# Shared keys and values of a hybrid decoder trunk: seven products of quarters (Strassen's scheme) in place of eight

## The chip, the cores and the metric

The kernel runs on 1 core of one Trainium2 chip. The metric is the device time of one launch in microseconds, median of several runs. A core has TensorE (PE, matrix products into PSUM banks), VectorE (DVE), ScalarE (ACT) and GpSimd (POOL) for elementwise work, and SyncE (SP), whose queue issues the DMA transfers here.

## The reference, cut to what matters

One HGRN2 layer updates the residual stream x; then the keys and values, shared by the FoX attention layer, are computed from it. The change lies in `h @ kv_w` (1024 x 1024 times 1024 x 4112; WIDTH is 2048, 16 heads of 128).

```python
def _shared_kv(x, c, kv_mod_w, kv_mod_b, kv_norm_g, kv_w, kv_fb, k_norm_g):
    ...
    h = _rms(x, kv_norm_g) * (1.0 + scale[:, None]) + shift[:, None]
    proj = h @ kv_w
    k = proj[..., :WIDTH].reshape(bsz, s, B_HEADS, HEAD_DIM)
    v = proj[..., WIDTH:2 * WIDTH].reshape(bsz, s, B_HEADS, HEAD_DIM)
    fl = proj[..., 2 * WIDTH:] + kv_fb
    k = _rms(k, k_norm_g).transpose(0, 2, 1, 3)
    ...
    F = jnp.cumsum(jax.nn.log_sigmoid(fl.astype(jnp.float32)), axis=1).transpose(0, 2, 1)
    return k, v, F
```

## The kernel before, in words

Every large float32 product is made of float32r halves: an operand is split into hi (ScalarE copies it with rounding, L224) and lo (VectorE or GpSimd subtracts hi from it, L225), and hi.hi + hi.lo + lo.hi are three matmuls into one bank. `halves` does both. On chip there are 25 blocks of 128 x 2048 floats, each of two halves of 1024; `renew` gives a block a new life, `ar(b, off, n)` names a piece.

The order of TensorE's work is written out by hand in a class `Weave`: matmuls are chained in the order in which the program issues them, `tick` counts a made-up time, and `spawn` lays side jobs (transposes and what follows) in when that time has come; `need(mark)` runs a side job at once. The other engines take their instructions in the order of a scheduler, SP's DMA queue too.

The stages: norm and HGRN2 with its input products; `out_proj`, which gives row tile t of the new residual stream in `a_done`; the shared keys and values; FoX attention with its own input products; a second `out_proj`. `a_done(t)` (L785) adds the residual row, stores it to x1d, squares it (L798), takes the root with a dozen small VectorE operations (`rsqrt_mean`, L213 to L219) and scales it on GpSimd (L800). `x_turn(t)` (L766), laid in 12 us of made-up time later, transposes the row tile in eight matmuls, stores it to xnd (L775), modulates it on VectorE (L776, L777) and splits it into halves in `hT`.

The stage in question is the loop over p (L873): for each of eight pairs of heads the products of k (four tiles of two row blocks, `gemm_N`, 24 matmuls of 128 x 256 per row block) and of v. k is read from its bank twice (L886, L888), squared sums are reduced (L887), the root taken, k scaled (L891), and `k_turn` transposes it and stores it to kd. v is copied (L902) and stored to vd. Weights are split one product set ahead by `split_w`, on GpSimd. For p = 0 the forget gate's 32 matmuls and its side job `forget_sums` follow. For the last p, `b_h` (L863) loads the transposed rows again from xnd, scales them on GpSimd (L868) and splits them anew as the operands of the FoX layer's products; those begin with L952, whose first tile is squared (L957), reduced (L959) and scaled (L961) before its transposes (`q_turn`). Names in the trace: blk is a block, mm, oa and sm are the three kinds of PSUM banks.

## Time and profile before

| what | value |
|---|---|
| median of 3 runs | 2383.89 us (2381.35 to 2388.03) |
| the profiled execution, its own time | 2386.32 us |
| its span | 2384.6 us |
| mean granted TensorE clock | 0.988 |
| TensorE busy | 96% of the span |
| VectorE, ScalarE, GpSimd busy | 58%, 42%, 25% |
| stage of shared keys and values | from about 1142.8 to 1548 us of the span |

The span is from the first to the last instruction of the execution; its own time holds 1.7 us more around it. In a timeline a row gives start, length, engine, line and operation; in brackets how long the engine stood idle before and what released it. A matmul's own length is longer than its pace, since matmuls overlap.

### The profile page before, as it was taken

To read this page: it belongs to the slowest core of one execution; us is meant where nothing else is said; L and a number is where in the kernel's file an instruction comes from. 1 tells how busy PE (TensorE), PEld (TensorE's weight loads), DVE (VectorE), ACT (ScalarE), POOL (GpSimd) and SP (SyncE) were. 2 spreads that over 40 slices of the span, in tenths; PEclk is the share of its full clock that TensorE was granted. 3 is DMA by queue.
4 is the path that set the end of the run, shared out by engine and by line. 5 is a ranking of instruction groups with operands and counts; after the bars stand their busy time and mean duration, and the time that the engine had idled before them with its cause. 6 is when DMAs were issued, how large, how long until landed. Compare 5 with 4: busy or idle time off the path is not lost.

```text
span 2384.6 us, 38476 instructions
## 1 busy us (share of the span) xinstructions
PE 2300.3 (96%) x14760; PEld 2063.2 (87%) x14760; DVE 1373.1 (58%) x3587; ACT 1004.1 (42%) x1646; POOL 587.4 (25%) x511
## 2 busy tenths in 40 slices
PE   4999999999999999999999999999999999999999
PEld 3888888888878798788999999989999999998887
DVE  7565555665656566647661131367767766777533
ACT  5453444434353526334422222344544545446321
POOL 3222222222222221101322121333333334333000
PEclk9999999999999999999999999999999999999999
DMA  8313131313222233666423232422222322235443
GB/s 270 102 40 103 45 97 45 97 53 98 63 80 75 77 94 98 200 198 190 147 82 94 71 95 84 141 67 74 81 80 67 94 70 91 66 95 173 155 142 117
DMA packets 219964, 244.95 MB, mean 103 GB/s; under 512 B 14546, under 2 KB 182644, under 8 KB 219780
## 3 DMA queue, kind: packets, MB, share of 16 engines
q1 hardware_dynamic: 219780, 242.49, 32.6%
q8 instruction: 116, 1.90, 0.3%
q14 instruction: 68, 0.56, 0.1%
HBM read 196.22 MB, written 46.21 MB: 102 GB/s over the span
## 4 chain that ended last, share of the span: by engine, by line
PE 82%; DVE 9%; ACT 4%; DMA 2%; issue 2%; POOL 1%; SPq 0%; DVEq 0%; ACTq 0%; POOLq 0%
PE mm L48 65%; PE oa L48 6%; PE sm L48 6%; PE sm L51 5%; DVE dl L471 1%; DVE blk L225 1%; DMA blk<-in_b_w_out_dram 1%; ACT L464 1%; DVE blk L465 1%; DVE rs_t L214 1%; ACT blk L224 1%; DVE blk L263 1%; ACT blk L464 0%; DVE blk L853 0%; POOL blk L225 0%
## 5 line engine op out<-in xcount | busy, mean ns | idle before, releaser
L48 PE MATMUL mm<-blk,blk 128*128 128x256 f32 (+1 forms) x10688 | 1916.0, 334 | 8.4 <-ACT blk L224 4.3
L48 PEld LDWEIGHTS mm<-blk,blk 128*128 128x128 f32 x10688 | 1604.0, 191 | 182.0 <-ACT blk L224 6.7
L224 ACT ACTIVATE blk<-blk 128x1024 fp32r<-128x1024 f32 (+3 forms) x352 | 304.8, 881 | 391.2 <-PE mm L48 251.3
L225 POOL TENSOR_TENSOR blk<-blk,blk 128x1024 fp32r<-128x1024 f32 (+1 forms) x134 | 312.6, 2343 | 569.5 <-ACT blk L224 567.0
L225 DVE TENSOR_TENSOR blk<-blk,blk 128x1024 fp32r<-128x1024 f32 (+3 forms) x218 | 204.2, 944 | 191.6 <-ACT blk L224 180.0
L48 PE MATMUL oa<-blk,blk 128*128 128x256 f32 (+1 forms) x1248 | 186.6, 286 | 25.2 <-DVE blk L515 14.7
L51 PE MATMUL sm<-ident,blk 128*128 128x128 f32 x1201 | 185.9, 275 | 23.7 <-DMA blk<-in_x_dram 9.8
L48 PE MATMUL sm<-blk,blk 128*128 128x128 f32 (+5 forms) x1408 | 207.5, 304 | 0.0
L48 PEld LDWEIGHTS oa<-blk,blk 128*128 128x128 f32 x1248 | 170.5, 194 | 36.7 <-DVE blk L515 16.0
L51 PEld LDWEIGHTS sm<-ident,blk 128*128 128x128 f32 x1201 | 142.6, 140 | 51.0 <-issue 20.2
L48 PEld LDWEIGHTS sm<-blk,blk 128*128 128x128 f32 (+1 forms) x1408 | 164.6, 171 | 19.6 <-issue 3.4
L1042 ACT ACTIVATE blk<-blk,m 128x128 f32<-128x128 f32 (+7 forms) x128 | 99.0, 773 | 128.2 <-DVE m L1040 115.8
L887 DVE TENSOR_REDUCE sst<-blk 128x4 f32<-128x512 f32 x32 | 21.8, 682 | 215.4 <-ACT blk L886 215.4
L1044 POOL TENSOR_SCALAR blk<-blk,smx 128x128 f32<-128x128 f32 (+7 forms) x128 | 97.6, 763 | 136.4 <-DVE smx L1043 117.3
L225 DVE TENSOR_TENSOR blk<-sm,blk 128x512 fp32r<-128x512 f32 (+1 forms) x160 | 93.0, 581 | 62.2 <-ACT blk L224 61.6
L263 DVE SCALAR_TENSOR_TENSOR blk<-blk,cc,blk 128x256 f32<-128x256 f32 x196 | 111.9, 573 | 20.2 <-DMA blk<-in_mod_w_dram 13.2
L1014 POOL TENSOR_TENSOR blk<-rows4k,keep 128x128 f32<-128x128 f32 x128 | 61.4, 479 | 238.2 <-DVE mx L1021 208.9
L545 POOL TENSOR_TENSOR blk<-blk,blk 128x512 f32<-128x512 f32 x32 | 43.0, 1344 | 237.8 <-ACT blk L544 210.4
L224 ACT ACTIVATE blk<-sm 128x512 fp32r<-128x512 f32 (+1 forms) x160 | 81.1, 507 | 46.9 <-PE sm L51 46.1
L1021 DVE CUSTOM_DVE_ANT_0 blk<-sm,rows4k 128x128 f32<-128x128 f32 (+3 forms) x176 | 84.7, 495 | 22.8 <-PE sm L48 21.4
L466 POOL TENSOR_SCALAR blk<-blk,cc 128x512 f32<-128x512 f32 x32 | 22.8, 712 | 260.0 <-ACT blk L463 253.4
L479 ACT ACT_TABLE_LOAD x31 | 39.8, 1283 | 102.4 <-DVE blk L474 102.4
(156 smaller groups left out, 1662.0 us busy)
## 6 DMA issues: line engine op xcount, KB each, us to landing
...
ogd<-blk SPq DMA_DIRECT2D x128, 64.0 KB, 1.8
...
```

The lines of the kernel that those rows point to most:

```text
L48: self._chain(self.PE.matmul(*a, **k))
L51: self._chain(self.PE.transpose(*a, **k))
L214: V.tensor_scalar(t.bitcast(I32), m.bitcast(I32), 1, None, ALU.logical_shift_right)
L224: S.activation(hi, src, AF.Copy)
L225: eng.tensor_tensor(lo, src, hi.bitcast(F32), ALU.subtract)
L263: V.scalar_tensor_tensor(acc, rawk(rb, k), csil[:, k:k + 1], acc, ALU.mult, ALU.add)
L479: S.activation(lf[:, :, 1, :], lf[:, :, 1, :], AF.Exp)
L545: G.tensor_tensor(u["ogT"], u["ogT"], sg(j, th), ALU.mult)
L1014: G.tensor_tensor(nfm, nF[:, i * P:n], negm, ALU.add)
L1021: V.tensor_tensor_reduce(dst, src, add, 1.0, -3e38, ALU.add, ALU.max, mx[:, nm:nm + 1])
L1042: S.activation(l[:, 0:n], l[:, 0:n], AF.Exp, bias=m, accum_out=sm)
L1044: G.tensor_scalar(l[:, 0:n], l[:, 0:n], sm, 0.0, ALU.mult, ALU.add)
```

## The change

The eight pairs become eight groups of 512 columns, four of v and four of k (`GROUPS`). Rows, contraction and columns are halved, so a group is a 2 x 2 by 2 x 2 product of quarters, and each quarter product is 4 row tiles x 4 steps of contraction x 3 matmuls = 48 matmuls of the shape used before. Seven products with sums (m = 1 to 7) take the place of eight: on the left A11, A12, S2 = A21 + A22 - A11, S3 = A11 - A21, S1 = A21 + A22, A22, S4 = A12 - S2; on the right B11, B21, T2 = B22 - T1, T3 = B22 - B12, T1 = B12 - B11, B21 - T2, B22. Left operands are made once: A11 and A12 in `x_turn` as before, the others from the modulated rows (blocks 4 to 7) on VectorE and, for S3, on GpSimd, while the first group's products run. Right operands are made per group: the four subtractions on GpSimd, the split on ScalarE and VectorE, for step i + 1 at the head of step i, into one of two slots (three from step 21). Sums of products are made in the bank where they can be, and else while the bank is read (`st_read`): ScalarE copies product 1 to SBUF, VectorE adds it, or an earlier sum, to the bank that it reads.

Step 0 needs x_turn of tiles 3 and 6; x_turn 7 is laid in after 8 instead of 12 us of made-up time. The forget gate's matmuls follow the first group and use A11, A12, S1 and A22 with weights changed to match; its arithmetic runs on 128 partitions. `b_h` comes in four parts at steps 1 to 4 of the last group, and `place` renames the blocks for the FoX stage, so that its operands lie where the group's operands have been used up.

```diff
+    GROUPS = [(kind, g) for kind, g in zip("vkkvvkkv", (0, 0, 1, 1, 2, 2, 3, 3))]
+    ORDER = [[1, 2, 6, 7, 5, 4, 3]] + [[1, 6, 2, 7, 5, 4, 3]] * 7
+    STEPS = [(n, m) for n in range(8) for m in ORDER[n]]
+    AOPS = {1: (0, 1), 2: (2, 3), 6: (14, 15), 7: (16, 17), 5: (18, 19), 4: (21, 22), 3: (4, 6)}
+    RAWQ = [(13, 0), (9, 0), (9, 1), (13, 1), (12, 0), (12, 1)]
...
+    def st_raw(n, q):
+        b, h = RAWQ[(4 * n + q) % 6]
+        return pr(b, 1024 * h, 1024)
...
+    def st_slot(i):
+        b = (8, 10)[i % 2] if i < 21 else (10, 7, 8)[i % 3]
+        return pr(b, 0, 1024, F32R), pr(b, 1024, 1024, F32R)
...
+    def st_prep(i):
+        n, m = STEPS[i]
+        b11, b12, b22, b21 = [st_raw(n, q) for q in range(4)]
+        t1, t2 = pr(23, 0, 1024), pr(23, 1024, 1024)
+        if m == 6:
+            G.tensor_tensor(t1, b12, b11, ALU.subtract)
+            G.tensor_tensor(t2, b22, t1, ALU.subtract)
+        if m == 7:
+            G.tensor_tensor(b12, b22, b12, ALU.subtract)
+        if m == 4:
+            G.tensor_tensor(t2, b21, t2, ALU.subtract)
+        halves(V, *st_slot(i), {1: b11, 2: b21, 3: b22, 4: t2, 5: t1, 6: t2, 7: b12}[m])
+    def st_products(i, banks, tiles):
+        m = STEPS[i][1]
+        wh, wl = [c256(w) for w in st_slot(i)]
+        first, last = m in (1, 6, 5), m in (2, 4, 3)
+        for j in tiles:
+            ps = c256(banks[j // 2])[:, j % 2, :]
+            for k in range(4):
+                ah, al = [a[:, k % 2, :] for a in st_A(AOPS[m][k // 2], j * P, P)]
+                for x, (lh, rh) in enumerate(((ah, wh), (ah, wl), (al, wh))):
+                    start = first and j % 2 == 0 and k == 0 and x == 0
+                    stop = last and j % 2 == 1 and k == 3 and x == 2
+                    PE.matmul(ps, lhsT=lh, rhs=rh[:, k, :], start=start, stop=stop, skip_group_check=True)
+                PE.tick(0.36)
...
-            raws["todo"] = [wcol(kv_w, o + p * 256) for p in range(NP) for o in (0, W)]
-            raws["slots"], raws["n"] = [13, 12], 0
-            raw_load()
+            for q in range(4):
+                st_load(0, q)
         if (ch, t) == (1, 4):
-            wnext.append(split_w(V, more=False))
+            st_prep(0)
...
             S.activation(xT, pt, AF.Copy)
             dma(xnd[th][:, q * 4:q * 4 + 4, o:o + P], c128(xT))
             V.tensor_tensor(c128(full), c128(xT), spread(g1[:, q * 4:q * 4 + 4], 4, P), ALU.mult)
-            V.tensor_tensor(c128(full), c128(full), spread(mcol[:, 48 + q * 4:52 + q * 4], 4, P), ALU.add)
             for k2 in range(2):
-                b = th * 4 + q * 2 + k2
-                halves(V, c512(ar(b, 0, 1024, F32R))[:, :, o:o + P], c512(ar(b, 1024, 1024, F32R))[:, :, o:o + P],
-                       c128(full)[:, 2 * k2:2 * k2 + 2, :])
+                hf = c512(pr(4 + 2 * th + q, 1024 * k2, 1024))[:, :, o:o + P]
+                c = 48 + q * 4 + k2 * 2
+                V.tensor_tensor(hf, c128(full)[:, 2 * k2:2 * k2 + 2, :], spread(mcol[:, c:c + 2], 2, P), ALU.add)
+                if th == 0:
+                    halves(V, *st_A(2 * q + k2, o, P), hf)
         PE.marks.add(("hkv", t))
         yield 0.0
@@ -798,127 +870,239 @@
         S.activation(xn, rows[t % 2], AF.Square, accum_out=ss)
         r = rsqrt_mean(ss, 1, 1.0 / D)
         G.tensor_scalar(xn, rows[t % 2], r, 0.0, ALU.mult, ALU.add)
-        PE.spawn(x_turn(t, xn), 12.0)
+        PE.spawn(x_turn(t, xn), 12.0 if t < NT - 1 else 8.0)
...
+    def st_sums(o, n):
+        for kk in range(2):
+            def hf(b):
+                return c512(pr(b, 1024 * kk, 1024))[:, :, o:o + n]
+            V.tensor_tensor(hf(22), hf(6), hf(7), ALU.add)
+            V.tensor_tensor(hf(12), hf(22), hf(4), ALU.subtract)
+    def st_split(src, dst, o=0, n=512):
+        for kk in range(2):
+            halves(V, *st_A(dst[kk], o, n), c512(pr(src, 1024 * kk, 1024))[:, :, o:o + n])
...
+    def st_done(n, c, tiles):
+        kind, g = GROUPS[n]
+        p, ts = 2 * g + c % 10 - 1, [4 * (c // 10 - 1), 4 * (c // 10 - 1) + 2]
+        if kind == "v":
+            for t, res in zip(ts, tiles):
+                dma(vd[p][:, t:t + 2, :], c256(res))
+            return
+        ss = sml.tile([P, 8], F32, name="ss8")
+        for b, res in enumerate(tiles):
+            sq = pr(5, 512 * b, 512)
+            S.activation(sq, res, AF.Square)
+            V.tensor_reduce(ss[:, 4 * b:4 * b + 4], c128(sq), AX.X, ALU.add)
+        r = rsqrt_mean(ss, 8, 1.0 / P)
+        for b, res in enumerate(tiles):
+            V.tensor_tensor(c128(res), c128(res), spread(r[:, 4 * b:4 * b + 4], 4, P), ALU.mult)
+        PE.spawn(k_turn(p, ts, tiles), 9.0)
+    def st_read(i, banks):
+        n, m = STEPS[i]
+        r1, u2, u3 = [[pr(blk, o + 512 * b, 512) for b in range(2)] for blk, o in ((11, 0), (11, 1024), (20, 0))]
+        if m == 1:
+            for b in range(2):
+                S.activation(r1[b], banks[b], AF.Copy)
+            return
+        if m in (6, 7):
+            for b in range(2):
+                V.tensor_tensor((u2 if m == 6 else u3)[b], banks[b], r1[b], ALU.add)
+            return
+        c = {2: 11, 5: 22, 4: 21, 3: 12}[m]
+        tiles = [st_res(c, b) for b in range(2)]
+        for b in range(2):
+            if m == 2:
+                S.activation(tiles[b], banks[b], AF.Copy)
+            else:
+                V.tensor_tensor(tiles[b], banks[b], {5: u3, 4: r1, 3: u2}[m][b], ALU.add)
+        if m == 3:
+            sq_n[0] += 2
+        st_done(n, c, tiles)
...
+    def b_h(th, k0):
+        for k in range(k0, k0 + 4):
+            xr = pr((9, 13)[k // 2 % 2], 1024 + 512 * (k % 2), 512)
             dma(xr, xnd[th][:, k, :])
             G.tensor_scalar(xr, xr, g1[:, 8 + k:9 + k], mcol[:, 24 + k:25 + k], ALU.mult, ALU.add)
             halves(V, hT(th, k, 0), hT(th, k, 1), xr)
...
-    raw_load()
-    wk = wnext[0]
-    for p in range(NP):
-        wv = split_w()
-        sst = sml.tile([P, 16], F32, name="sst")
-        for t in range(0, NT, 2):
-            if p == 0:
-                PE.need(("hkv", t + 1))
-            ps = mm_ps()
-            gemm_N(ps, wk, t)
-            sq = unit((t // 2) % 2)
-            S.activation(sq, ps, AF.Square)
-            V.tensor_reduce(sst[:, t * 2:t * 2 + 4], c128(sq), AX.X, ALU.add)
-            S.activation(kr(t), ps, AF.Copy)
-        r = rsqrt_mean(sst, 16, 1.0 / P)
-        for t in range(0, NT, 2):
-            V.tensor_tensor(c128(kr(t)), c128(kr(t)), spread(r[:, 2 * t:2 * t + 4], 4, P), ALU.mult)
-        PE.spawn(k_turn(p, kr), 11.0 if p == 1 else 6.0)
-        if p == NP - 1:
+    LAST = len(STEPS) - 7
+    for i, (n, m) in enumerate(STEPS):
+        if i == 0:
+            PE.need(("hkv", 3))
+            PE.need(("hkv", 6))
+            st_prep(1)
+        if i >= 1:
+            st_prep(i + 1)
+        if i == 1:
+            st_sums(0, 384)
+            st_split(12, AOPS[6], 0, 384)
+        if i == 2:
+            PE.need(("hkv", 7))
+            st_sums(384, 128)
+            st_split(12, AOPS[6], 384, 128)
+            for kk in range(2):
+                G.tensor_tensor(pr(6, 1024 * kk, 1024), pr(4, 1024 * kk, 1024), pr(6, 1024 * kk, 1024), ALU.subtract)
+            st_split(6, AOPS[7])
+        if i == 3:
+            st_split(22, AOPS[5])
+            renew(22)
+        if i == 4:
+            st_split(7, AOPS[4])
+            for kk in range(2):
+                V.tensor_tensor(pr(5, 1024 * kk, 1024), pr(5, 1024 * kk, 1024), pr(12, 1024 * kk, 1024), ALU.subtract)
+            renew(4, 6)
+            st_split(5, AOPS[3])
+            fls = forget_weights()
...
+        if i == LAST + 1:
+            place.update(zip(range(25), (0, 1, 14, 15, 2, 3, 16, 17, 18, 19, 8, 10, 12, 13, 21, 22, 4, 6, 5, 7, 9, 23, 20,
+                                         11, 24)))
+            b_h(0, 0)
+        if i == LAST + 2:
+            b_h(0, 4)
+        if i == LAST + 3:
+            b_h(1, 0)
+        if i == LAST + 4:
             raws["todo"] = [wcol(bw, o + q * 256) for q in range(NP) for o in (0, W)]
-            raws["slots"], raws["n"] = [12], 0
+            raws["slots"], raws["n"], wn[0] = [12], 0, 0
             raw_load()
-        wk = split_w()
-        for t in range(0, NT, 2):
-            ps = mm_ps()
-            gemm_N(ps, wv, t)
-            vt = unit(4 + (t // 2) % 2)
-            S.activation(vt, ps, AF.Copy)
-            dma(vd[p][:, t:t + 2, :], c256(vt))
-            if p == NP - 1 and t in (2, 6):
-                b_h(t // 4)
...
+            b_h(1, 4)
+        if i == LAST + 5:
+            wk = split_w()
+        banks = st_banks(m)
+        st_products(i, banks, range(4))
+        st_read(i, banks)
+        if i == 6:
+            PE.spawn(forget_sums(forget_logits(fls)), 2.0)
     PE.drain()
```

TensorE at the entry of the stage, before: the last matmuls of the projection, x_turn 5, and the first products; then, 99 matmuls on, x_turn 6.

```order
L48 MATMUL mm<-blk_0_7655,blk_1_7660 128x512
L51 MATMUL sm<-ident,blk_1_118 128x128 x8
L48 MATMUL mm<-blk_0_85,blk_0_69 128x256
L48 MATMUL mm<-blk_0_87,blk_0_69 128x256
...
L48 MATMUL mm<-blk_0_85,blk_1_78 128x256
L51 MATMUL sm<-ident,blk_0_117 128x128 x8
L48 MATMUL mm<-blk_0_85,blk_0_77 128x256
```

The same place in the change:

```order
L48 MATMUL mm<-blk_0_7657,blk_1_7662 128x512
L51 MATMUL sm<-ident,blk_1_118 128x128 x8
L51 MATMUL sm<-ident,blk_0_117 128x128 x8
L48 MATMUL oa<-blk_0_85,blk_0_69 128x256
L48 MATMUL oa<-blk_1_86,blk_0_69 128x256
```

x_turn 6 has moved from behind 99 matmuls to ahead of the first one, next to x_turn 5.

GpSimd during the first group of the change (L872 is the scaling in a_done, L786 to L791 the right-hand subtractions of `st_prep`, L1059 S3):

```order
L872 TENSOR_SCALAR blk24_0_117<-blk23_0_115,rs_y_9118 128x1024
L786 TENSOR_TENSOR blk23_0_115<-blk9_0_8366,blk13_0_95 128x1024
L872 TENSOR_SCALAR blk24_1_118<-blk23_1_116,rs_y_9168 128x1024
L789 TENSOR_TENSOR blk9_0_8366<-blk9_1_8367,blk9_0_8366 128x1024
L787 TENSOR_TENSOR blk23_1_116<-blk9_1_8367,blk23_0_115 128x1024
L791 TENSOR_TENSOR blk23_1_116<-blk13_1_96,blk23_1_116 128x1024
L1059 TENSOR_TENSOR blk6_0_8362<-blk4_0_8358,blk6_0_8362 128x1024
L1059 TENSOR_TENSOR blk6_1_8363<-blk4_1_8359,blk6_1_8363 128x1024
```

Before, the scalings of tiles 5, 6 and 7 (L800) had the weight splits of the first v products (L225) among them; now the subtractions of the first group stand there, two of S3 last.

GpSimd at the exit, before (L868 is the scaling in `b_h`, L225 the split of the FoX weights, L1014 the first work of attention):

```order
L868 TENSOR_SCALAR blk23_1_116<-blk23_1_116,cc_177 128x512 x2
L225 TENSOR_TENSOR blk11_0_91<-blk12_0_93,blk10_0_89 128x1024
L868 TENSOR_SCALAR blk23_0_115<-blk23_0_115,cc_177 128x512
L225 TENSOR_TENSOR blk11_1_92<-blk12_1_94,blk10_1_90 128x1024
L868 TENSOR_SCALAR blk23_0_115<-blk23_0_115,cc_177 128x512
L868 TENSOR_SCALAR blk23_1_116<-blk23_1_116,cc_177 128x512 x2
```

And in the change (L1036 is the scaling in `b_h`, L233 the split of the FoX weights):

```order
L1036 TENSOR_SCALAR blk13_1_96<-blk13_1_96,cc_179 128x512 x2
L786 TENSOR_TENSOR blk23_0_115<-blk12_1_94,blk12_0_93 128x1024
L789 TENSOR_TENSOR blk12_1_94<-blk13_0_95,blk12_1_94 128x1024
L787 TENSOR_TENSOR blk23_1_116<-blk13_0_95,blk23_0_115 128x1024
L1036 TENSOR_SCALAR blk9_1_8367<-blk9_1_8367,cc_179 128x512 x2
L791 TENSOR_TENSOR blk23_1_116<-blk9_0_8366,blk23_1_116 128x1024
```

The scalings now begin among the last group's own subtractions and are all ahead of the FoX weights' splits; before, the last of them came after those of the first gate weight.

## Rows read from the trace of the kernel before

**Rows 1.** The page's part 1: busy time, share, instructions.
```profile
PE 2300.3 (96%) x14760; PEld 2063.2 (87%) x14760; DVE 1373.1 (58%) x3587; ACT 1004.1 (42%) x1646; POOL 587.4 (25%) x511
```

**Rows 2.** Busy time by stretch: stretch, length, PE, PEld, DVE, ACT, POOL, clock, DMA, GB/s.
```profile
1300.00:1350.00 50.00, 49.31 (x414) 49.11 (x413) 10.15 (x20) 14.47 (x22) 10.79 (x5) 1.00 0.27 85
...
1550.00:1575.00 25.00, 20.03 (x150) 19.81 (x150) 16.83 (x51) 7.16 (x14) 7.47 (x7) 0.86 0.20 63
```

**Rows 3.** Timeline of ScalarE, middle of the stage: reads of successive banks.
```profile
1306.04 0.60 ACT L886 ACTIVATE blk<-mm 128x512 f32<-128x512 f32 x1 [4.17 <-PE mm L48]
1311.80 0.60 ACT L886 ACTIVATE blk<-mm 128x512 f32<-128x512 f32 x1 [4.67 <-PE mm L48]
...
1354.74 0.60 ACT L886 ACTIVATE blk<-mm 128x512 f32<-128x512 f32 x1 [4.17 <-PE mm L48]
```

**Rows 4.** Timeline of TensorE at the entry of the stage.
```profile
1142.02 1.03 PE L51 MATMUL sm<-ident,blk 128*128 128x128 f32 x8
1142.82 12.12 PE L48 MATMUL mm<-blk,blk 128*128 128x256 f32 x99
1154.77 1.04 PE L51 MATMUL sm<-ident,blk 128*128 128x128 f32 x8
```

**Rows 5.** Timelines of VectorE and GpSimd at the entry: the norms of tiles 5 to 7.
```profile
1145.74 0.69 DVE L790 TENSOR_TENSOR blk<-blk,rows4k 128x512 f32<-128x512 f32 x1 [2.77 <-DMA blk<-in_x_dram]
...
1149.02 2.39 DVE L219 SCALAR_TENSOR_TENSOR rs_y<-rs_t,rs_y 128x1 f32<-128x1 f32 x1
...
1135.93 2.40 POOL L225 TENSOR_TENSOR blk<-blk,blk 128x1024 fp32r<-128x1024 f32 x1 [9.39 <-ACT blk L224]
...
1148.65 2.73 POOL L225 TENSOR_TENSOR blk<-blk,blk 128x1024 fp32r<-128x1024 f32 x1 [7.10 <-ACT blk L224]
1153.51 1.12 POOL L800 TENSOR_SCALAR blk<-blk,rs_y 128x1024 f32<-128x1024 f32 x1 [2.12 <-DVE rs_y L215]
```

**Rows 6.** Timelines of GpSimd and VectorE where both work at once.
```profile
1139.19 1.48 POOL L800 TENSOR_SCALAR blk<-blk,rs_y 128x1024 f32<-128x1024 f32 x1 [0.85 <-DVE rs_y L219]
...
1168.93 4.82 POOL L225 TENSOR_TENSOR blk<-blk,blk 128x1024 fp32r<-128x1024 f32 x2 [5.36 <-ACT blk L224]
...
1139.82 0.69 DVE L789 TENSOR_TENSOR rows4k<-mm,rows4k 128x512 f32<-128x512 f32 x1
...
1169.86 0.69 DVE L887 TENSOR_REDUCE sst<-blk 128x4 f32<-128x512 f32 x1 [1.98 <-ACT blk L886]
...
1171.40 2.37 DVE L214 TENSOR_SCALAR rs_t<-rs_m 128x16 int32<-128x16 int32 x1
```

**Rows 7.** Groups by line and form from 1250 to 1500 us: count, busy us, mean ns, idle before.
```profile
L225 POOL TENSOR_TENSOR blk<-blk,blk 128x1024 fp32r<-128x1024 f32 x22 | 52.4, 2405 | 184.5 <-ACT blk L224 184.5
L224 ACT ACTIVATE blk<-blk 128x1024 fp32r<-128x1024 f32 x23 | 24.3, 1057 | 35.7 <-PE mm L48 22.6 <-issue 13.1
```

**Rows 8.** Timeline of VectorE: a split of 1024, of 256 columns, and two small operations.
```profile
1122.47 0.42 DVE L225 TENSOR_TENSOR blk<-blk,blk 128x256 fp32r<-128x256 f32 x1
...
1124.32 1.23 DVE L225 TENSOR_TENSOR blk<-blk,blk 128x1024 fp32r<-128x1024 f32 x1
...
1328.11 0.17 DVE L217 SCALAR_TENSOR_TENSOR rs_t<-rs_y 128x16 f32<-128x16 f32 x1
1328.32 0.17 DVE L218 TENSOR_TENSOR rs_t<-rs_t,rs_m 128x16 f32<-128x16 f32 x1
```

**Rows 9.** Waits from 1145 to 1560 us: total, times, longest.
```profile
PE sm L51 <- DVE blk L891: 6.1, 8, 1.4
```

**Rows 10.** Timelines of TensorE and VectorE at the exit of the stage.
```profile
1562.39 1.08 PE L51 MATMUL sm<-ident,blk 128*128 128x128 f32 x4 [4.97 <-DVE blk L961]
1563.13 7.66 PE L48 MATMUL mm<-blk,blk 128*128 128x256 f32 x48
...
1570.98 5.92 PE L48 MATMUL mm<-blk,blk 128*128 128x256 f32 x39
...
1557.78 0.69 DVE L225 TENSOR_TENSOR blk<-blk,blk 128x512 fp32r<-128x512 f32 x1 [0.16 <-ACT blk L224]
```

More of the change, by code (lines that the diff above doesn't have):

```diff
@@ L104, in renew, with pr @@
             i, js = i if isinstance(i, tuple) else (i, (0, 1))
+            i = place.get(i, i)
             for j in js:
                 blocks[i, j] = arena.tile([P, 1024], F32, tag=f"blk{i}_{j}", name=f"blk{i}_{j}")
-    renew(*range(25))
-    def ar(b, off, n, dt=F32):
+    place = {}
+    def pr(b, off, n, dt=F32):
         t = blocks[b, off // 1024]
@@ L116, in ar @@
         return t[:, off:off + n]
+    renew(*range(25))
+    def ar(b, off, n, dt=F32):
+        return pr(place.get(b, b), off, n, dt)
     def unit(u, n=512, dt=F32):
@@ L136, in hybrid_trunk_kernel @@
     Fd = drm.tile([H, T], F32, name="Fd")
+    zd = [drm.tile([P, P], F32, name=f"zd{i}") for i in range(2)]
     gd = [drm.tile([KT, P], F32, name=f"gd{l}") for l in range(2)]
@@ new lines, in forget_logits @@
+    def forget_logits(fls):
+        pf = [sm_ps(), sm_ps()]
+        for th, terms in enumerate(([(k, (0, 1, 2, 3)[k // 2], k) for k in range(8)],
+                                    [(k, (18, 19)[k // 2], k) for k in range(4)]
+                                    + [(8 + k, (21, 22)[k // 2], k) for k in range(4)])):
+            for x, (w, blk, k) in enumerate(terms):
+                for lo in range(2):
+                    PE.matmul(pf[th][0:48, :], lhsT=fls[:, w, :], rhs=st_A(blk, 0, 512)[lo][:, k % 2, :],
+                              start=(x + lo == 0), stop=(x + lo == 8))
+                PE.tick(0.46)
+        return pf
@@ L839, in forget_sums @@
+        dma(zd[0].rearrange("(h s) q -> h (s q)", h=H), z0)
+        z, e, a, s2, acc = [rows4k[:, i * P:(i + 1) * P] for i in range(5)]
+        dma(z, zd[0])
         yield 20.0
@@ L842, in forget_sums @@
         S.activation(e, e, AF.Exp)
[L843 removed]
+        V.tensor_scalar(a, e, 1.0, 2.0, ALU.mult, ALU.add)
+        V.reciprocal(a, a)
         yield 3.0
[L845 to L847 removed]
         V.tensor_tensor(a, a, e, ALU.mult)
         V.tensor_tensor(s2, a, a, ALU.mult)
[L850 removed]
         V.tensor_scalar(acc, s2, 1.0 / 17, None, ALU.mult)
@@ L853, in forget_sums @@
             V.scalar_tensor_tensor(acc, acc, 1.0 / n, s2, ALU.add, ALU.mult)
-            yield 3.0
+        yield 3.0
         V.scalar_tensor_tensor(acc, acc, 1.0, a, ALU.add, ALU.mult)
         V.tensor_scalar(z, z, -1.0, 0.0, ALU.mult, ALU.max)
-        yield 3.0
         V.scalar_tensor_tensor(z, acc, 2.0, z, ALU.mult, ALU.add)
+        dma(zd[1], z)
+        renew((7, (0,)))
+        one, out_f = pr(7, 0, 1024)[0:H, :], rows4k[0:H, :]
         G.memset(one, 1.0)
-        V.tensor_tensor_scan(e, one, z, 0.0, ALU.mult, ALU.add)
-        dma(Fd, e)
-    def b_h(th):
-        for k in range(KT):
-            xr = unit(20 + k % 4)
+        dma(z0, zd[1].rearrange("(h s) q -> h (s q)", h=H))
+        yield 10.0
+        V.tensor_tensor_scan(out_f, one, z0, 0.0, ALU.mult, ALU.add)
+        dma(Fd, out_f)
+        PE.marks.add("F")
+        yield 0.0
+    def b_h(th, k0):
+        for k in range(k0, k0 + 4):
+            xr = pr((9, 13)[k // 2 % 2], 1024 + 512 * (k % 2), 512)
             dma(xr, xnd[th][:, k, :])
@@ new lines, in hybrid_trunk_kernel @@
+    fls = None
+    for i, (n, m) in enumerate(STEPS):
[5 more added lines that the diff above has]
+            st_prep(i + 1)
+        if i == 20:
+            PE.need("F")
+            renew(7)
+        if i == 1:
[18 more added lines that the diff above has]
+            fls = forget_weights()
+        x = i - 7 * n
+        if n + 1 < len(GROUPS):
+            if x in ((4, 5) if n == 0 else (0, 1)):
+                st_load(n + 1, x - (4 if n == 0 else 0))
+            if x == 3 and n > 0:
+                st_load(n + 1, 2)
+            if x == 5 and n > 0:
+                st_load(n + 1, 3)
+            if x == 6 and n == 0:
+                st_load(n + 1, 2)
+                st_load(n + 1, 3)
+        if i == LAST + 1:
[7 more added lines that the diff above has]
+        if i == LAST + 4:
```

83 lines of the change are left out of this document (46 added, 37 removed).

## The prediction

> **What bounds the kernel now.** I read the page's first part, then the busy time by stretch, then the timelines around the stage that changes. TensorE is busy for 2300 of 2384.6 us [rows 1]; inside the stage a stretch of 50 us holds 49.31 us of it at the full granted clock [rows 2]. So the stage's time is the number of its products times their pace, plus the few places where TensorE waits. The pace: two ScalarE reads of successive banks start at 1306.04 and 1311.80, with 48 matmuls between, so 5.76/48 = 0.120 us each; a whole pair of heads (384 matmuls, 16 transposes) repeats after 48.70 us [rows 3]. The places are three: the entry, where x_turn of tiles 6 and 7 is laid between the first products [rows 4]; the transposes of k, which wait for the scaling at L891 eight times, 6.1 us in all [rows 9]; and the exit, where TensorE stands still for 4.97 us [rows 10].
>
> **Products removed.** Each of the eight groups of 512 columns had 384 matmuls and now has 7 x 48 = 336, of the same shape and operand kinds. 8 x 48 = 384 fewer at 0.120 us: **-46.1**. The transposes (128 for k, 16 in the last two x_turns) and the 32 matmuls of the forget gate stay. The Trainium skill, TensorE: Matmul & The Clock Gate (Back-to-back issue gap), puts a lone stream of 256 columns at 256/2.4 + 2.5 = 109 ns. By that the saving would be 41.9 and the sum 4.2 later; the pace in the rows is measured with the weight loads of this very form, so I use the rows.
>
> **The entry: before the first product.** Before, 99 matmuls run between x_turn 5 and x_turn 6 [rows 4]. Now x_turn 6 stands ahead of the first product (first place of the order), so TensorE waits for tile 6's norm with nothing to do. In the trace x_turn 5 ends where the products start, at 1142.82, and x_turn 6 can start at 1154.77: 11.95 us, the upper end. In that stretch the chain of tile 6 was held twice by a GpSimd weight split, which the change does not issue there: L219 took 2.39 us until the split of 1148.65 ended, and the split of 1135.93 to 1138.33 held the norm of tile 5, after which the row load for tile 7 may start, on which VectorE then stands 2.77 us [rows 5]. Without both: 11.95 - 2.4 - 2.4 = 7.2. The lower end is the chain with no wait in it: two operations of 0.69, the square (1.06, as ScalarE's pass over 1024 [rows 7]), a dozen small operations at 0.21 [rows 8] and the scaling, 1.12 [rows 5], 6.1 from 1139.82 [rows 6], of which 3.0 lie before 1142.82: 3. I take **+7.2**.
>
> **The first group.** Before, all operands were made during the projection ahead. Now five of seven left operands are made while the first products run. Here it matters that VectorE and GpSimd hinder each other: a VectorE operation that would take 0.17 us took 2.37 us, until GpSimd's second subtraction was over; a reduction with one input (0.69 us at 1169.86), and an operation that reads a bank (L789, 0.69 us), ran beside GpSimd undisturbed [rows 6]. So work with two operands in SBUF goes one after the other with GpSimd's.
> GpSimd, until the last left operand is there (second place of the order): six subtractions at 2.40 [rows 7] and one norm at 1.12 [rows 5], 15.5.
> VectorE, until the operands of the seventh product are there: ten left-operand halves, five right-operand halves, four sums (in two pieces each, 384 and 128 columns) and two differences, 21 pieces of 1024 at 1.23 [rows 8] = 25.8; two x_turns, each 2 x 0.69 [rows 6] + 4 x 0.42 [rows 8] = 3.1, so 6.1; six bank reads at 0.69 = 4.1. Sum 36.0, with GpSimd's 51.5.
> TensorE needs 6 x 5.76 + 0.9 = 35.5 until its seventh product. So that product is 16 late if all is serial, 0.5 if GpSimd hides entirely; waits of one engine on another can add 8 to the upper end. The ends are 0.5 and 24; the rows show exactly these forms as serial, so I take **+15.5**. ScalarE's half of a split (1.06 [rows 7]) lies beside this.
>
> **The later groups.** A k group asks of VectorE seven right-operand halves, 8.6; ten bank reads and eight reductions at 0.69, 12.4; eight scalings, 5.5; four chains of twelve small operations at 0.21, 10.1: 36.6. GpSimd adds four subtractions, 9.6; if all of it were serial, 46.2. TensorE takes 7 x 5.76 and 32 transposes at about 0.11 (eight in 0.80 [rows 4]), 43.8. Bank reads and reductions run beside GpSimd, so the sum fits, but only just, and the first k group also carries the forget gate's arithmetic. Ends: 0, and 6 per group where a chain is stopped at each step. I take 2.5 for each of four groups, 10, and take off the 6.1 that the waits on L891 cost now: **+4**, from -6 to +18. A v group asks 15.5 of VectorE and 9.6 of GpSimd in 40.3: nothing. Four loads of 512 KB a group take the place of four, so SP and the DMA engines have no more to carry.
>
> **The exit.** Here TensorE waits 4.97 us for L961, which stands behind the last halves of b_h on VectorE (L225 at 1557.78), and then runs slower: 48 matmuls take 7.66 instead of 5.76, the next 39 take 5.92 instead of 4.7, with a mean granted clock of 0.86 in that stretch [rows 2, 10]. That is 8.1. The change issues the same 16 scalings and splits one to four products earlier (third place of the order), up to four products ahead of need, 23 us. What is late next is the first gate weight, whose split on GpSimd can hold the first small operations; I leave 0.6 for it: **-7.5**, from -8.1 to 0.
>
> **The clock.** A wait of 7 us at the entry should cost what 4.97 us cost at the exit, 3.1, but while VectorE is behind, a slower TensorE loses nothing; half: **+1.5**, from 0 to 3.
>
> **Sum.** -46.1 + 7.2 + 15.5 + 4 - 7.5 + 1.5 = -25.4. The profiled execution took 2386.3 (span 2384.6), 2.4 over the median of the runs; 2386.3 - 25.4 = 2360.9, against the median **2358.5**.
>
> **Rivals.**
> *The start is hidden.* If VectorE finds its turn beside GpSimd, the first group costs 2 instead of 15.5: 2345. For it: GpSimd's subtractions need loads that may come at other moments. Against it: rows 6. Chance 0.20.
> *TensorE stays at a lower clock through the first group,* since it waits before most of its products. At the pace of rows 10, 7.66/48 = 0.160, its 336 matmuls take 13.4 more, of which about half would hide: 2365. For it the row at 0.86; against it that 0.7 us waits elsewhere left the clock full. The Trainium skill, TensorE: Matmul & The Clock Gate (HAM oscillation), speaks against the change here: short idle times between bursts send the array back to half pace each time. By that, at 256/1.2 = 213 ns, the group would take 31 more; no row of this kernel shows a stretch as slow as that. Chance 0.08.
> *The k groups are VectorE's.* If each k group takes 5 us more than I allow (serial, with blocked small operations like the 2.37 us one [rows 6]): 2379, no change that can be told. Chance 0.09.
> *Slower: the two weight slots become a chain.* Operand i+1 may only be written when product i-1 has ended, as it takes its slot, and must be there 5.76 later. In a k step what can stand ahead of its VectorE half is two reads, two reductions, a chain and two scalings, 1.4 + 1.4 + 2.5 + 1.4 = 6.7, and a block of 2.4; with 1.06 and 1.23 that makes 11.4, so 5.6 late. There are 16 such steps; from 1.6 each beyond my allowance the gain is gone, at 2.4 each the time is 2397. For it: in such steps VectorE's work is longer than a product. Against it: the reads wait for the banks, so the half usually goes first, and from step 21 on there are three slots. Chance 0.09.
> That the scheme is not what is issued can be left out: the order has 384 rows of matmuls fewer.
>
> **How the numbers follow.** The forecast has 0.54. A measurement tells about 0.3%, 7 us, from no change. Forecast, hidden start and lower clock are faster: 0.82; the k groups make 0.09 of no change, the chain 0.09 of slower. The range goes from 2338 (hidden start, with the k groups at their lower end) to 2381 (the k groups' case); outside lie the chain and the far ends.
>
> **What would show it.** Matmuls of the stage at 0.120 us. No product for some 7 us after x_turn 5, with TensorE released by GpSimd's scaling. In the next 50 us waits of TensorE on VectorE halves (S2, then S3) of some 15 us, VectorE operations of 2 to 3 us ending where GpSimd's end. At the exit no wait on L961's successor above 1 us, and the clock full. It would be wrong if the entry ran without waits, if the 0.120 changed, or if the k groups took much over 44 us each.

## The result, and the profile after

| | median | range | runs |
|---|---|---|---|
| before | 2386.98 us | 2381.35 to 2388.03 | 5 |
| changed | 2373.63 us | 2370.02 to 2375.41 | 5 |

The ratio is 0.9946, with a 95% interval from 0.993 to 0.9962: 13 us faster, where 25 had been forecast (2358.5 against 2383.89). Measured a second time, beside another kernel, the ratio was 0.9937 (0.9924 to 0.9951). The kernel before has a median of 2386.98 over five runs, 3.1 above the 2383.89 of three from which the forecast counted. The profiled execution has a span of 2369.2 us against 2384.6, 15.4 less; that difference is taken apart here.

Part 1 of the page, for [rows 1]: TensorE has 384 matmuls fewer and 37 us less busy time, VectorE 128 us more.

```profile
PE 2263.2 (96%) x14376; PEld 2026.4 (86%) x14376; DVE 1501.3 (63%) x3838; ACT 1016.6 (43%) x1634; POOL 601.9 (25%) x514
```

Busy time by stretch in the changed kernel, for [rows 2] (stretch, length, PE, PEld, DVE, ACT, POOL, clock, DMA, GB/s):

```profile
1140.00:1160.00 20.00, 14.09 (x94) 13.45 (x94) 19.00 (x43) 5.11 (x9) 9.88 (x5) 0.83 0.38 109
1160.00:1180.00 20.00, 11.12 (x75) 10.51 (x74) 19.48 (x21) 11.04 (x16) 7.75 (x3) 0.84 0.24 80
1180.00:1200.00 20.00, 19.20 (x137) 18.93 (x137) 17.82 (x20) 7.16 (x8) 1.89 (x1) 0.82 0.31 100
1350.00:1400.00 50.00, 50.00 (x419) 50.00 (x418) 19.87 (x22) 11.70 (x13) 12.01 (x5) 1.00 0.33 115
```

In the first 40 us VectorE is the full engine (38.5 us of 40) and TensorE waits at a granted clock between its two levels; in a v group later TensorE is busy without a gap at the full clock, 419 matmuls in 50 us, 0.119 us each. Timeline of TensorE from the entry, for [rows 4]:

```profile
1141.27 1.03 PE L51 MATMUL sm<-ident,blk 128*128 128x128 f32 x8
1148.16 1.97 PE L51 MATMUL sm<-ident,blk 128*128 128x128 f32 x8 [5.86 <-POOL blk L872]
1149.78 9.97 PE L48 MATMUL oa<-blk,blk 128*128 128x256 f32 x69
...
1163.85 4.40 PE L48 MATMUL oa<-blk,blk 128*128 128x256 f32 x24 [2.87 <-ACT blk L940]
...
1174.43 0.51 PE L48 MATMUL mm<-blk,blk 128*128 128x256 f32 x2 [1.86 <-ACT blk L232]
1179.08 2.50 PE L48 MATMUL mm<-blk,blk 128*128 128x256 f32 x10 [4.14 <-DVE blk L233]
1182.38 11.00 PE L48 MATMUL mm<-blk,blk 128*128 128x256 f32 x72 [0.80 <-DVE blk L944]
...
1204.73 10.43 PE L48 MATMUL sm<-blk,blk 128*128 128x256 f32 x56
1215.01 1.23 PE L48 MATMUL oa<-blk,blk 128*128 128x256 f32 x9
```

The first wait is x_turn 6 behind GpSimd's scaling of tile 6 (L872); the waits of 1160 to 1182, 9.7 us in all, are those of the sums. From the first product (1149.78) to the next group's (1215.01) it is 65.23 us. 336 products at 0.120, x_turn 7 (0.80) and the forget gate's 32 matmuls (1204.73 to 1215.01 less 24 at 0.120, 7.4) make 48.5: the first group is 16.7 late, 9.7 of it in waits and 7.0 in matmuls slower than 0.120.

The k groups, for [rows 9]: the last part of the row gives the idle time before the transposes, and 12.6 of it stands at L931, the scaling of k. The first k group has 7.75 of these; VectorE's and GpSimd's timelines show why:

```profile
L51 PE MATMUL sm<-ident,blk 128*128 128x128 f32 x1201 | 187.8, 277 | 36.2 <-DVE blk L931 12.6 <-DMA blk<-in_x_dram 9.6 <-POOL blk L872 5.9
```
```profile
1235.36 2.40 POOL L786 TENSOR_TENSOR blk<-blk,blk 128x1024 f32<-128x1024 f32 x1 [19.18 <-DMA blk<-zd]
1237.84 4.31 POOL L789 TENSOR_TENSOR blk<-blk,blk 128x1024 f32<-128x1024 f32 x1
1245.07 2.34 POOL L787 TENSOR_TENSOR blk<-blk,blk 128x1024 f32<-128x1024 f32 x1 [2.92 <-DVE rs_y L227]
...
1236.39 1.40 DVE L221 TENSOR_SCALAR rs_m<-ss 128x8 f32<-128x8 f32 x1
1237.70 2.27 DVE L1026 TENSOR_TENSOR_SCAN rows4k<-blk,blk 16x1024 f32<-16x1024 f32 x1
1239.90 2.27 DVE L222 TENSOR_SCALAR rs_t<-rs_m 128x8 int32<-128x8 int32 x1
...
1245.10 2.33 DVE L225 SCALAR_TENSOR_TENSOR rs_t<-rs_y 128x8 f32<-128x8 f32 x1
...
1248.35 1.28 DVE L931 TENSOR_TENSOR blk<-blk,rs_y 128x512 f32<-128x512 f32 x2
```

Of the twelve small operations (0.17 each elsewhere) three last 1.40, 2.27 and 2.33, ending where GpSimd's subtractions end, and the forget gate's prefix sum (L1026) stands between two of them: 12 us from L221 to L931, where twelve at 0.21 make 2.5. A GpSimd subtraction that met VectorE's work lasts 4.31 instead of 2.40.

The exit, for [rows 10], TensorE first, then ScalarE, SP's queue and VectorE:

```profile
1527.59 13.84 PE L48 MATMUL mm<-blk,blk 128*128 128x256 f32 x114
1546.97 1.09 PE L51 MATMUL sm<-ident,blk 128*128 128x128 f32 x4 [5.54 <-DVE blk L1145]
1547.71 8.08 PE L48 MATMUL mm<-blk,blk 128*128 128x256 f32 x48
...
1561.72 0.60 PE L51 MATMUL sm<-ident,blk 128*128 128x128 f32 x4
...
1540.51 1.06 ACT L232 ACTIVATE blk<-blk 128x1024 fp32r<-128x1024 f32 x1 [10.22 <-DMA blk<-vd]
1541.48 1.07 ACT L1141 ACTIVATE blk<-mm 128x512 f32<-128x512 f32 x2
...
1533.63 0.38 SPq L244 DMA_DIRECT2D blk<-in_b_w_in_dram  x1
...
1534.61 0.61 SPq L1175 DMA_DIRECT2D blk<-vd  x1
...
1528.73 2.60 DVE L233 TENSOR_TENSOR blk<-blk,blk 128x1024 fp32r<-128x1024 f32 x1 [6.01 <-ACT blk L232]
...
1541.60 1.45 DVE L233 TENSOR_TENSOR blk<-blk,blk 128x1024 fp32r<-128x1024 f32 x1 [9.07 <-ACT blk L232]
```

The wait is there as before, 5.54 us, with the lower clock behind it. ScalarE stood 10.22 us for head 0's values (L1175, the load in `fox_v`), and the square of the first q tiles (L1141), whose bank had been full since about 1533.4 (48 products into the row of 1527.59), came right behind. VectorE's queue stood the same way. The load itself went out late: its buffer was the one of head 0's keys, whose split on VectorE (L233 at 1528.73) ended at 1531.33, and after that SP's queue stood on a weight load (L244 at 1533.63) that waited for GpSimd's split of the gate weight. Two more rows of the kernel before set the bounds of that stretch:

```profile
1535.22 22.20 PE L48 MATMUL mm<-blk,blk 128*128 128x256 f32 x183
...
1576.74 0.60 PE L51 MATMUL sm<-ident,blk 128*128 128x128 f32 x4
```

There the last 114 of 183 matmuls are the q products; they begin at about 1557.42 - 13.84 = 1543.6. From the first q product to the third q_turn it was 33.1 us before and is 34.1 now; from the end of x_turn 5 to the first q product 400.8 before, 385.5 now; x_turn 5 itself ends 0.75 earlier. Together -15.1 of the 15.4.

### The profile page after: what moved, and what is told of

It is laid out like the page before. It is cut to its first block, busy times and chain, and to the rows that moved or that the text cites. A ratio compares the mean times of both kernels' runs of the same rounds, so it can differ in the third digit from the quotient of the medians.

```text
span 2369.2 us, 38021 instructions
## 1 busy us (share of the span) xinstructions
PE 2263.2 (96%) x14376; PEld 2026.4 (86%) x14376; DVE 1501.3 (63%) x3838; ACT 1016.6 (43%) x1634; POOL 601.9 (25%) x514
## 4 chain that ended last, share of the span: by engine, by line
PE 73%; DVE 11%; ACT 6%; issue 4%; DMA 4%; POOL 1%; SPq 0%; ACTq 0%; DVEq 0%; POOLq 0%
PE mm L48 53%; PE oa L48 8%; PE sm L48 7%; PE sm L51 5%; DVE blk L233 2%; DVE blk L271 1%; DVE dl L479 1%; ACT blk L232 1%; DVE blk L473 1%; ACT L472 1%; DMA blk<-in_mod_w_dram 1%; ACT L487 1%; ACT blk L472 1%; POOL blk L233 1%; ACT L470 1%
## 5 line engine op out<-in xcount | busy, mean ns | idle before, releaser
L48 PE MATMUL mm<-blk,blk 128*128 128x512 f32 (+1 forms) x9120 | 1726.0, 343 | 15.2 <-DVE blk L233 7.9
L48 PEld LDWEIGHTS mm<-blk,blk 128*128 128x128 f32 x9120 | 1419.5, 192 | 185.9 <-DVE blk L233 10.5
L232 ACT ACTIVATE blk<-blk 128x1024 fp32r<-128x1024 f32 (+3 forms) x372 | 335.4, 914 | 461.2 <-PE mm L48 281.1
L233 DVE TENSOR_TENSOR blk<-blk,blk 128x1024 fp32r<-128x1024 f32 (+3 forms) x268 | 276.2, 1039 | 228.8 <-ACT blk L232 225.2
L233 POOL TENSOR_TENSOR blk<-blk,blk 128x1024 fp32r<-128x1024 f32 (+1 forms) x104 | 240.0, 2314 | 308.6 <-ACT blk L232 302.5
L48 PE MATMUL oa<-blk,blk 128*128 128x256 f32 (+1 forms) x2016 | 286.4, 287 | 27.8 <-DVE blk L523 14.7
L48 PEld LDWEIGHTS oa<-blk,blk 128*128 128x128 f32 x2016 | 267.4, 196 | 39.2 <-DVE blk L523 16.0
L48 PE MATMUL sm<-blk,blk 128*128 128x256 f32 (+6 forms) x1824 | 269.2, 303 | 0.1
L48 PEld LDWEIGHTS sm<-blk,blk 128*128 128x128 f32 (+2 forms) x1824 | 218.2, 175 | 23.2 <-issue 3.5
L51 PE MATMUL sm<-ident,blk 128*128 128x128 f32 x1201 | 187.8, 277 | 36.2 <-DVE blk L931 12.6
L233 DVE TENSOR_TENSOR blk<-sm,blk 128x512 fp32r<-128x512 f32 (+1 forms) x160 | 92.9, 581 | 62.7 <-ACT blk L232 62.2
L473 DVE TENSOR_TENSOR_SCAN blk<-rows4k,blk 128x512 f32<-128x512 f32 x32 | 39.1, 1223 | 70.3 <-ACT blk L472 70.3
```

Source lines behind the costliest of these rows:

```text
L48: self._chain(self.PE.matmul(*a, **k))
L51: self._chain(self.PE.transpose(*a, **k))
L232: S.activation(hi, src, AF.Copy)
L233: eng.tensor_tensor(lo, src, hi.bitcast(F32), ALU.subtract)
L473: V.tensor_tensor_scan(u["b"], rst, u["lf"], 0.0, ALU.mult, ALU.add)
```

## The experiments

Times are medians; each ratio is to runs of the kernel before on the same chip, where that had 2383.5 to 2387.0. The changed kernel has 0.9937 to 0.9946 in this measure. Three questions: what holds the exit, whether VectorE's and GpSimd's work in the first group goes one after the other, and what makes the k groups wait.

### Exit: the norm of q ahead of head 0's values

```diff
-        halves(V, ar(15, 0, 1024, F32R), ar(15, 1024, 1024, F32R), raw)
+        hi = S.activation(ar(15, 0, 1024, F32R), raw, AF.Copy)
+        if h == 0:
+            behind(hi, q_last[0])
+        V.tensor_tensor(ar(15, 1024, 1024, F32R), raw, ar(15, 0, 1024, F32R).bitcast(F32), ALU.subtract)
```

`behind` stands here for a longer call that gives the scheduler an order of two instructions; `q_last[0]` is the scaling of the latest q tiles (L1145).

> The changed kernel with one order edit: the first half of head 0's values (ScalarE, then VectorE) is put behind the norm of the first q tiles instead of ahead of it. Same instructions. The changed kernel alone has 2373.6 and a wait of 5.54 us of TensorE at the exit, on L1145. Theory (the norm stands in ScalarE's and VectorE's queues behind a half whose data is still on its way): the wait falls under 0.6, and the 87 products behind it come back from 13.98 us towards 10.5, so 2365 to 2368. Rival A (GpSimd's weight split of that moment holds the small operations of the norm): a wait of 2 to 3 stays, 2371. Rival B (the exit is not on the path, head 0 gets its values later and gives the time back): 2373.

2364.61, ratio 0.9914 (0.9901 to 0.9928). Timeline of TensorE at the exit of this kernel:

```profile
1528.74 13.85 PE L48 MATMUL mm<-blk,blk 128*128 128x256 f32 x114
1542.43 0.60 PE L51 MATMUL sm<-ident,blk 128*128 128x128 f32 x4
1542.78 5.99 PE L48 MATMUL mm<-blk,blk 128*128 128x256 f32 x48
...
1548.97 5.92 PE L48 MATMUL mm<-blk,blk 128*128 128x256 f32 x39
1554.72 0.60 PE L51 MATMUL sm<-ident,blk 128*128 128x128 f32 x4
```

No wait is left, and 48 matmuls take 5.99 instead of 8.08. The third q_turn comes 26.0 us after the first q product instead of 34.1: the exit was worth 8 in this stretch, and the theory holds. By the ratios (0.9914 against 0.9937 and 0.9946) the whole kernel gained 5.5 to 7.6. One number of the expectation, and of the prediction, was wrong: the 39 matmuls take 5.92 us here too. Nine of them are 512 wide (30 x 0.12 + 9 x 0.24 = 5.8), so [rows 10] held no slower clock in that row.

### Exit: a buffer of its own for head 0's values

```diff
-        raw = ar(13, 0, 1024)
+        raw = ar(13, 1024 if h == 0 else 0, 1024)
```

> The changed kernel with head 0's values loaded into a buffer of their own instead of the one that its keys have just left. The half of the values still stands ahead of the norm of q on ScalarE, but its load no longer waits for the keys' split. Theory (the exit's wait is late data behind a shared buffer, seen through an engine's queue): the wait of 5.54 us falls under 1.5 and the result is that of the order edit, ratio to the kernel before 0.990 to 0.9925. Rival (whatever stands ahead of the norm there costs it, data or not): half or less of it, ratio 0.9935 to 0.9955.

2366.66, ratio 0.9917 (0.9903 to 0.993); the changed kernel beside it 2371.06:

> The changed kernel itself once more, beside the one with the buffer: ratio to the kernel before 0.993 to 0.996, as measured first, so that the gains of the edits can be set against it.

The half still stands ahead of the square, but its load, issued 7.0 us behind the first q product before, now goes out 6.7 ahead of it, and TensorE passes without a wait. SP's queue and TensorE in this kernel:

```profile
1524.57 0.61 SPq L1175 DMA_DIRECT2D blk<-vd  x1
```
```profile
1531.30 13.84 PE L48 MATMUL mm<-blk,blk 128*128 128x256 f32 x114
1544.98 0.60 PE L51 MATMUL sm<-ident,blk 128*128 128x128 f32 x4
```

The medians are 4.4 apart, and all four times lie under all five of the changed kernel (2365.55 to 2367.73 against 2370.2 to 2375.84). The spans of the profiled executions (2366.0 and 2374.1) are 8.1 apart, but that of the changed kernel is its slowest. So it is not the place in ScalarE's queue alone but the late load. What made it late has two parts: the buffer, held by the keys until 1531.33 (their split ran against GpSimd's weight split and took 2.60 us), and the weight load ahead of it in SP's queue, which waited until 1533.63. The edit took both away at once, since with its own buffer the load goes out ahead of the weight loads; how much each weighs stays open.

### Exit of the kernel before

```diff
-                b_h(t // 4)
+                b_h(t // 4, range(6 if t == 6 else KT))
...
+            if p + t == 0:
+                b_h(1, (6, 7), scaled)
```

> The kernel before, with one order edit: the last four halves of b_h (k 6 and 7 of the second half of the rows) come behind the norm of the first q tiles on ScalarE and VectorE; same instructions. In the kernel before TensorE waits 4.97 us there, then runs slower. Theory (the exit's cost is the norm standing in the queues behind halves whose data is late, in this kernel as in the changed one): the wait falls under 1.5 us and the time by 5 to 8, ratio to the kernel before 0.9965 to 0.998. Rival (the halves themselves are the last to come, since GpSimd scales until 1557.1, and products then wait for them instead): ratio 0.999 to 1.001.

2384.07, ratio 0.9987 (0.9978 to 0.9996): 3 us, less than the theory's 5 to 8 and more than the rival's, with an interval that reaches into both. Timeline of TensorE:

```profile
1537.05 22.20 PE L48 MATMUL mm<-blk,blk 128*128 128x256 f32 x183
1562.40 0.63 PE L51 MATMUL sm<-ident,blk 128*128 128x128 f32 x4 [3.15 <-DVE blk L966]
```

The wait falls from 4.97 to 3.15. By the trace the rest stands on the halves of b_h still ahead of the norm (k 4 and 5), which wait for GpSimd (2.94 us just ahead of the square): it has two weight splits of 2.41 to do between its scalings. In this kernel, then, both seem to hold: the order, which this run shows, and halves that are late in themselves, which the trace suggests and no run tested.

### First group: without the right-hand subtractions

```diff
+        if n == 0 and m > 3:
+            halves(V, *st_slot(i), {4: b21, 5: b12, 6: b22, 7: b12}[m])
+            return
         if m == 6:
```

> The changed kernel without the four subtractions on GpSimd for the right operands of the first group (four of 2.40 us); each product there takes an untouched quarter, so this group's results are others. Theory (two-operand work of VectorE and GpSimd goes one after the other, so GpSimd's time is in the sum): the seven products of the first group end 9.6 us earlier, from 16.7 late to about 7, total 2363 to 2366. Rival (VectorE's own work bounds the group and GpSimd's is hidden): 2372 to 2374.

2365.66, ratio 0.9915 (0.9902 to 0.9929). From first product to next group 58.83 us (1152.60 to 1211.43), 6.4 less than 65.23, not 9.6. By the trace, what GpSimd still does, two subtractions for S3, takes the place of the rest. Timeline of GpSimd:

```profile
1167.09 8.41 POOL L1062 TENSOR_TENSOR blk<-blk,blk 128x1024 f32<-128x1024 f32 x2 [14.00 <-DVE blk L893]
```

Two operations of 2.40 take 8.41 us while VectorE works, and the next product waits 5.85 for the split behind them.

### First group: the subtractions on VectorE

```diff
-            G.tensor_tensor(t1, b12, b11, ALU.subtract)
+            V.tensor_tensor(t1, b12, b11, ALU.subtract)
...
```

> The changed kernel with all 34 subtractions of GpSimd for operands moved to VectorE, where one takes about 1.23 us instead of 2.40. Theory (serial): the first group gains 6 x 1.17 = 7, and the four k groups, where 9.6 of GpSimd become 4.9 of VectorE, lose some of their 12.6 us of waits: 2362 to 2367. Rival (GpSimd's time is hidden): six more operations of 1.23 on VectorE make the first group 7.4 longer and the k groups' waits grow: 2380 to 2390.

> The changed kernel with only the first group's six subtractions on VectorE (four for right operands, two for a left one); the later groups keep theirs on GpSimd. Theory: the first group comes out as with all of them moved (54.4 us from its first product to the next group's, instead of 65.2), and the k groups wait as in the changed kernel (12.6 in all): 2361 to 2364. Rival (what was gained in the first group is lost again at the first k group, whose wait moves with the forget gate's arithmetic): 2368 to 2371.

All moved: 2365.69, ratio 0.9905 (0.9891 to 0.9919). Only the first group's six: 2363.32, ratio 0.9911 (0.9897 to 0.9925), whose timeline of TensorE is

```profile
1151.18 10.20 PE L48 MATMUL oa<-blk,blk 128*128 128x256 f32 x69
...
1173.28 8.97 PE L48 MATMUL mm<-blk,blk 128*128 128x256 f32 x72 [1.84 <-DVE blk L945]
...
1192.29 3.00 PE L48 MATMUL mm<-blk,blk 128*128 128x256 f32 x23 [1.28 <-DVE blk L233]
...
1205.40 0.87 PE L48 MATMUL oa<-blk,blk 128*128 128x256 f32 x6
```

54.22 us, 11.0 less: more work on the engine that is behind makes the group shorter. Of the 11.0, 7.0 was expected from 6 x (2.40 - 1.23); with fewer waits the clock came back too (72 matmuls in 8.97 instead of 11.00). In the k groups it does not pay: their waits grew from 12.6 to 15.2 us in all, with 5.89 in the second one, where four moved subtractions now stand between the small operations of the norm.

The Trainium skill, SBUF — State Buffer (SBUF: two separate sides), says that VectorE, with two inputs in SBUF or in a two-port mode, and GpSimd share a pair of ports under an exclusive lock. The trace agrees in that either engine's operation stands: VectorE's L225, which reads rs_y as both of its inputs (2.33 us for 8 columns), GpSimd's subtraction beside VectorE's work (4.31). An operation with one input stood too (L222, 2.27); no row shows whether it ran in such a mode.

### Entry: x_turn 6 behind the first product

```diff
-            PE.need(("hkv", 6))
             st_prep(1)
...
         if i == 1:
+            PE.need(("hkv", 6))
```

> The changed kernel with the transposes of x_turn 6 behind the first product instead of ahead of it (8 transposes moved past 48 products, no other instruction moved). Theory (VectorE is behind through the first group, so an earlier start of the first product only makes the next waits longer): the entry wait of 5.86 us goes, the waits in the 40 us after it grow by as much, 2373 to 2374. Rival (the entry wait is on the path): 2367 to 2368.

2370.75, ratio 0.9934 (0.9921 to 0.9946). Timeline of TensorE:

```profile
1144.37 5.99 PE L48 MATMUL oa<-blk,blk 128*128 128x256 f32 x48
...
1164.88 0.80 PE L48 MATMUL mm<-blk,blk 128*128 128x256 f32 x2 [5.09 <-ACT blk L232]
1169.37 5.69 PE L48 MATMUL mm<-blk,blk 128*128 128x256 f32 x34 [3.70 <-DVE blk L233]
...
1180.45 12.59 PE L48 MATMUL mm<-blk,blk 128*128 128x256 f32 x82 [4.62 <-DVE blk L233]
```

The first product starts 7.7 us sooner after x_turn 5, and waits of 5.09, 3.70 and 4.62 come instead. From x_turn 5 to the next group it is 71.1 us (1143.58 to 1214.67) against 73.7: most of the 7.7 is lost again. The time lies between the two ranges and by the intervals cannot be told from that of the changed kernel. So the theory holds in the main: VectorE sets the end of this group.

### k groups: an order, and all together

```diff
-            G.tensor_tensor(t1, b12, b11, ALU.subtract)
+            late(G.tensor_tensor(t1, b12, b11, ALU.subtract))
...
-        V.tensor_tensor_scan(out_f, one, z0, 0.0, ALU.mult, ALU.add)
+        scan = V.tensor_tensor_scan(out_f, one, z0, 0.0, ALU.mult, ALU.add)
+        behind(scan, k11[1])
```

`k11[n]` is the scaling (L931) of a k group's first result, and `late` puts the next group's four subtractions behind it.

> The changed kernel with an order of its k groups: the prefix sum of the forget gate, and the next group's GpSimd subtractions, come behind the norm of a k group's first result instead of into the middle of its twelve small operations. Theory (the 7.75 us wait on L931 is that chain held three times by a GpSimd subtraction and once by the prefix sum of 2.27): the chain takes about 2.6 us instead of 13, the wait falls under 1 and the 2.00 of the second k group goes, with some of the slower clock behind them: 2363 to 2367. Rival (the subtractions pushed back are then late for the next group, whose products wait): 2370 to 2376.

2370.23, ratio 0.9935 (0.9921 to 0.9948): at the edge of the rival's range, and no gain over the changed kernel that the intervals show. The first wait is gone, the norm takes 2.9 us, but the timeline of TensorE has others:

```profile
1258.76 0.84 PE L51 MATMUL sm<-ident,blk 128*128 128x128 f32 x4 [1.93 <-DVE blk L944]
1301.92 0.38 PE L48 MATMUL mm<-blk,blk 128*128 128x256 f32 x1 [0.88 <-ACT blk L232]
...
1547.86 1.09 PE L51 MATMUL sm<-ident,blk 128*128 128x128 f32 x4 [5.43 <-DVE blk L1160]
```

The prefix sum, met by a subtraction, lasts 3.88 in the next norm, and the v group's subtractions, held back, make its products wait 0.88 and 2.87. Less the exit's wait, next group to q_turn takes 324.4 us (1218.03 to 1547.86 less 5.43) instead of 326.4: of 8 to be had 6 went elsewhere.

> The norm of q first, the first group's subtractions on VectorE and the order of the k groups, all three in the changed kernel. If each works on a wait of its own the gains add: 9 for the exit, 10 for the first group, 8 for the k groups: 2345 to 2350. If they share one (VectorE late all through the stage), less than two thirds of it: over 2355.

2353.42, ratio 0.9871 (0.9857 to 0.9884): between the two ranges. Under the changed kernel that is 16 to 18 us by the ratios. One by one, in the same measure, the edits gave 5.5 to 7.6, 6 to 8 and 0.5 to 2.6, together 12 to 19. So the gains add as they were measured, but they are less than the 27 that was expected of them, since the order of the k groups brought little.

> As the one with three edits, and the transposes of x_turn 6 behind the first product. With VectorE no longer the last in the first group, the entry wait of 5.86 us should now be on the path and this edit worth 4 to 6: 2340 to 2345. Rival (VectorE still sets the end of the first group): no more than the 2.9 that it gave alone: 2344 to 2350.

2353.48, ratio 0.9869 (0.9856 to 0.9883): above both ranges, but the entry gave nothing here, so the rival's account holds, though in the profiled executions its span was 2.7 shorter.

> As the one with three edits, but of the later groups only the second k group's subtractions are held back (not the v group's behind it, whose product then waited 2.9 us at the lower clock), and the prefix sum comes behind the second norm of the k group instead of the first. Theory (those two places were the rest of what the k-group edit gave back): no wait above 2 us between the first group and the exit, 2347 to 2351. Rival (the waits only move to the next chain): 2352 to 2356.

2355.0, ratio 0.9865 (0.985 to 0.988): in the rival's range. The prefix sum (L1041) does come behind the second norm, whose scaling is L945 at 1241.50, but now it stands in the third one, which is held by a GpSimd subtraction as well and whose scaling releases TensorE. VectorE, then TensorE:

```profile
1241.50 1.29 DVE L945 TENSOR_TENSOR blk<-blk,rs_y 128x512 f32<-128x512 f32 x2
...
1244.51 2.27 DVE L1041 TENSOR_TENSOR_SCAN rows4k<-blk,blk 16x1024 f32<-16x1024 f32 x1
...
1254.31 1.09 PE L51 MATMUL sm<-ident,blk 128*128 128x128 f32 x4 [5.17 <-DVE blk L945]
```

So the wait only moved to the next chain. The last three kernels beat both the kernel before and the changed one, and these runs cannot tell them apart; where the rest of the k groups' wait can go stays open.

## Why the prediction was right and wrong

- **Products removed, -46.1: right.** 384 fewer, at 0.119 to 0.120 us in the stretches without a wait.
- **Entry, +7.2: right.** The first product comes 7.7 us after x_turn 5, of which x_turn 6's own matmuls, which ran later before, are 0.8: 6.9. That it was not worth saving ("while VectorE is behind") showed when it was taken away.
- **First group and its clock, 15.5 + 1.5: the sum right, at 16.7, its parts not.** The text looked for some 15 us of waits and 1.5 of clock; it was 9.7 of waits and 7.0 of slower products. The lower clock of the first group, a rival at 0.08, did happen (72 matmuls in 11.00 instead of 8.97), inside that sum, as VectorE's work sets the end. That this work goes one after the other with GpSimd's held in direction: six subtractions on VectorE gave 11.0 where 7.0 was expected, leaving four out gave 6.4 where 9.6 was. The rows cited for it show only small operations held; pieces of 1024 are held too (2.60 us at 1528.73 instead of 1.23).
- **Later k groups, +4: low.** Waits on L931 are 12.6 against 6.1, so +6.5; the first k group alone waits 7.75. The text named the forget gate there, but priced nothing for it. Its own sign of being wrong, a k group much over 44 us, came for the first two: 51.3 and 48.8, then 42.1 and 44.6.
- These four make -16.0; -15.3 was measured from x_turn 5 to the first q product, against -17.9 forecast for them. 0.7 is not accounted for.
- **Exit, -7.5: wrong, +1.0 measured. This is the step that failed.** It took the wait for a property of its cause in the old kernel, late halves of b_h; the change did issue those earlier, and they no longer held anything. But the wait was of whatever stands ahead of the norm of q on ScalarE and VectorE with late data, and the next thing there was the half of head 0's values, whose load came late, behind the keys' buffer and a weight load in SP's queue. The text asked what is late next and answered with the gate weight, at 0.6, for the small operations that its split might hold; those ran at 0.17 each. That split did hold the weight load ahead of the values. Where the half was put behind, or loaded early, the stretch from the first q product to the third q_turn fell from 34.1 to 26.0, the gain forecast; the whole kernel gained 4 to 8. A part of the term's working was wrong as well: the 1.2 us read as slower clock in 39 matmuls are their width.

The forecast with the exit as measured, -25.4 + 7.5 + 1.0 = -16.9, would have stood against -15.4. The range (2338 to 2381) held the result; the rivals did not contain what happened, since none was about the exit.
